# Listing experts in groups of three blocks, halving mask chunks on POOL, and an output tile finished in steps

## The chip, the cores and the metric

The kernel runs on one core of a Trainium2 chip. The metric is the device time of one execution in microseconds (us), as the median of several runs. A profile of one execution, with its trace, tells what each engine did.

## The reference

Two transformer blocks are applied to 256 tokens of width 2048. The change lies in the last part of the second block, a mixture of 16384 single-vector experts with product keys, and in the norm behind it. Each token picks 16 experts for each of 8 heads, so 128 of them:

```
s1, s2 = q[..., :half] @ keys1, q[..., half:] @ keys2
expert, gate = top 16 of all sums of the two top 16 lists, softmax
z = einsum('cd,ced->ce', x, u[expert])
out = einsum('ce,ced->cd', gelu(z) * gate, v[expert])
result = rmsnorm(x + out, norm_final_g)
```

The kernel does not gather `u`: it multiplies all tokens with all 16384 rows of `u`. Of `v` it reads only those rows that some token picked.

## The kernel before

All large products go through one stream of items. An item is a 1 MB weight tile (`raw`, three buffers, loaded on the SP queue) of two halves, and each half is a half-step of the loop in `stream`. In half-step k, ACT cuts the upper part of half k+3 (`whi`, L414), then `step` runs background tasks, then DVE cuts the rest of half k+3 (`wlo`, L421, which also issues the load of a later item), and then PE multiplies half k (L465 and L466: eight products of 512 columns and eight of 256). All engines take their instructions in the order in which they are written, so a background instruction stands at a fixed place between the cuts and products.

`step` deals out background work by a credit: each half-step adds 1.3, a task's `yield c` takes |c| away, a yield of zero or above ends the task's turn in this half-step, and a negative one lets it go on while credit is left. A debt is carried over.

In the part at hand the stream's items are numbered by the 128 tiles of `peer_u` (merged form, L465 and L466), half-step 2i for the first half of tile i, and after them 108 items of `v` (L1645 to L1647). Behind each second tile of `peer_u`, `post_u` closes the pair: ACT copies part of the result (L335), DVE does two operations (L338, L339), ACT a Gelu (L1566) and a store of 256 KB to the table `zg` in memory.

`mask_task(ti)` runs for each 128 tokens; for the second 128 it begins at tile 96, half-step 192. It loads the gates, 128 x 128 cells for 128 tokens, in eight chunks of 1 MB (`vraw<-zg`, L1424, four buffers, on the SP queue between the loads of `raw`), and DVE reduces each with a maximum (L1434). For the second half, `list_task` follows. From the masks it makes three classes of experts (picked by the first tokens only, by both, by the second only), of at most 29, 50 and 29 blocks of 128 list places. A scan on DVE and a small product on PE (L1452) give each picked expert its place. Then pieces of up to five blocks (`PIECE`) are made: POOL (L1489) and DVE (L1490) make a one-hot of the places, PE multiplies it with the counts in groups of at most three blocks (L1504, into one of two PSUM banks `bg`), and the group is evicted. For the first two classes ACT copies a row (L1517) and does one Sign with a sum for each block (L1519); for the third DVE compares and sums (L1510 to L1514). At the end the list positions are ready (L1529), and a flag is set.

`row_source(v)` gathers the rows of `v` by the lists, on POOL's queue (L1603). It is called seven items ahead. If the flag is not set by then, it calls `step` until it is, so that all that is left of the lists is written at one place: ahead of PE's half-step 240. `fetch` gathers rows of `zg` (L1611, six buffers, `ROWS`), and `weigh` multiplies them. PE sums both output tiles in PSUM. The last five items belong to the second tile alone; at the first of them `finish_tile(0)` writes the whole end of the first tile at once: four squares on ACT, the root, four scalings on ACT, four products with the gain on POOL, four stores. `finish_tile(1)` does the same for the second tile after the last item, with DVE for the scaling.

Of the kernel before, what the change touches and what calls it, by code (L numbers as in the profile page):

```python
# [8 lines left out]
F32R = mybir.dt.float32r  # L9
# [5 lines left out]
ALU = mybir.AluOpType  # L15
AX = mybir.AxisListType

P = 128
# [27 lines left out]
    "consts2": [("keep", 384), ("cen", 128)],  # L46
    "consts3": [("tri", 128), ("slots", 640), ("past", 128), ("row", 2), ("starts", 24)],
}
# [3 lines left out]
NLIST = sum(CAPS)  # L52
PIECE = 5
DUMMY = P * P
# [3 lines left out]
EARLY = 3  # L58
ROWS = 6
COEF = 6  # L60
# [15 lines left out]
def constants():  # L76
    c = {}
    r = np.arange(P)
    c["ident"] = np.eye(P)
    half, rot = 8, 16  # L80
    inv = np.power(np.float32(500000.0), -np.arange(half, dtype=np.float32) * np.float32(2.0) / np.float32(rot))
    ang = np.arange(TOK, dtype=np.float32)[None, :] * inv.astype(np.float32)[:, None]
    cos, sin = np.ones((P, TOK)), np.zeros((P, TOK))
    prot = np.zeros((P, P))
    for b in (0, 64):
        for i in range(half):
            cos[b + i] = cos[b + half + i] = np.cos(ang[i])
            sin[b + i] = sin[b + half + i] = np.sin(ang[i])
            prot[b + half + i, b + i] = -1.0
            prot[b + i, b + half + i] = 1.0  # L90
    c["cos"], c["sin"], c["prot"] = cos, sin, prot
    c["blk"] = (r[:, None] // 64 == r[None, :] // 64)
    c["iota"] = np.broadcast_to(r[None, :], (P, P))
    q, k = r[:, None], r[None, :]
    c["keep"] = np.concatenate([k <= q, np.ones((P, P), bool), k <= q], 1)
    c["win"] = np.where(np.concatenate([k <= q, k > q, k <= q], 1), 0.0, NEG)
    cen = np.zeros((P, P))
    for m in range(P):
        cen[:64, m] = -1.0 / 64
        cen[m % 64, m] += 1.0  # L100
    c["cen"] = cen
    c["tri"] = r[:, None] < r[None, :]
    c["slots"] = np.broadcast_to(np.arange(640)[None, :], (P, 640))
    c["past"] = np.zeros((P, P))
    for at, n in zip(CLASS_AT, CAPS):
        c["past"][:, at:at + n] = P * np.arange(n)[None, :] + r[:, None] + 0.5 - P * n / 2
    c["past"][:, :CLASS_AT[2]] *= -1.0
    starts = [P * b for n in CAPS for b in range(0, n, PIECE)]
    c["starts"] = np.broadcast_to(np.array(starts + [0] * (24 - len(starts)))[None, :], (P, 24))
    c["row"] = np.stack([(r - 128.0) * 128.0, 0.0 * r], 1)  # L110
    return {g: np.ascontiguousarray(np.concatenate([c[n].astype(np.float32) for n, _ in items], 1))
            for g, items in _CONSTS.items()}
# [133 lines left out]
class Build:  # L246
# [988 lines left out]
    def peer(self):  # L1235
# [144 lines left out]
        def begin_lists():  # L1380
# [17 lines left out]
            for name, (o, w) in offsets.items():  # L1398
                self.cons[name] = c3[:, o:o + w]
            st["abs"], st["gt"] = cut(2, 640), cut(2, 3, P)  # L1400
            st["hot"], st["prer"] = self.t([2, 640], "hot", dt=F32R), self.t([3, 132], "pre", dt=F32R)
            st["scratch"] = t[:, 0:at[0]]
            st["m"], st["cls"], st["pre"] = cut(2, P), cut(3, P), cut(3, 132)
            st["n"], st["mid"], st["half"], st["end"] = (cut(3) for _ in range(4))
            st["bias"], st["high"] = cut(24), cut(24)
            st["sum"], st["row"], st["rho"] = cut(NLIST), cut(NLIST), cut(NLIST)
# [8 lines left out]
        def mask_task(ti):  # L1415
# [13 lines left out]
            for g in range(3):  # L1429
                load(g)  # L1430
                yield 0.0
            for g in range(8):
                load(g + 3)
                V.tensor_reduce(st["m"][:, ti, 16 * g:16 * g + 16], chunks[g], axis=AX.X, op=ALU.max)  # L1434
                yield 2.3
            V.tensor_scalar(st["m"][:, ti], st["m"][:, ti], 0.0, None, op0=ALU.is_gt)
# [4 lines left out]
        def list_task():  # L1441
# [7 lines left out]
            V.tensor_copy(st["n"], pre[:, :, P - 1])  # L1449
            yield 2.2  # L1450
            ps = self.bg1()
# [5 lines left out]
            for c in range(3):  # L1457
                V.tensor_scalar(pre[:, c, 0:P], pre[:, c, 0:P], ps[:, c:c + 1], -64.0 * CAPS[c], op0=ALU.add, op1=ALU.add)
            V.tensor_scalar(st["prer"][:, :, 0:P], pre[:, :, 0:P], 4096.0, None, op0=ALU.min)
            V.tensor_copy(st["prer"][:, :, P:P + 2], self.con("row")[:, None, :].to_broadcast([P, 3, 2]))  # L1460
            over = st["bias"][:, 0:3]
# [3 lines left out]
            V.tensor_copy(st["over"][:, 0:1], over[:, 0:1])  # L1465
            yield 2.6
            pieces = [(c, b, min(PIECE, CAPS[c] - b)) for c in range(3) for b in range(0, CAPS[c], PIECE)]
            signs, counts = [p for p in pieces if p[0] < 2], [p for p in pieces if p[0] == 2]
            pieces = []
            while signs or counts:  # L1470
                pieces += signs[:3] + counts[:1]
                del signs[:3], counts[:1]
            lo, hi = st["bias"], st["high"]
# [19 lines left out]
            hot(0)  # L1493
            yield -1.0
            for i, (c, b, n) in enumerate(pieces):
                if i + 1 < len(pieces):
                    hot(i + 1)
                    yield -0.6
                for j0 in range(0, n, 3):
                    ps = self.bg1()  # L1500
                    m = min(3, n - j0)
                    for j in range(m):
                        o = (j0 + j) * P
                        T.matmul(ps[:, 132 * j:132 * j + 130], st["hot"][:, i % 2, o:o + P], st["prer"][:, c, 0:130],  # L1504
                                 start=True, stop=True)
                    yield 0.0
                    col = CLASS_AT[c] + b + j0
                    pv = ps[:, 0:396].rearrange("p (b k) -> p b k", k=132)
                    if c == 2:
                        V.tensor_copy(st["row"][:, col:col + m], pv[:, 0:m, P])  # L1510
                        gt = st["gt"][:, j0 // 3 % 2, 0:m]
                        V.tensor_tensor(gt, pv[:, 0:m, 0:P], self.con("past", col, col + m)[:, :, None].to_broadcast([P, m, P]),
                                        op=ALU.is_gt)
                        V.tensor_reduce(st["sum"][:, col:col + m], gt, axis=AX.X, op=ALU.add)  # L1514
                        yield -1.2
                        continue
                    S.activation(st["row"][:, col:col + m], pv[:, 0:m, P], AF.Copy)  # L1517
                    for j in range(m):
                        S.activation(pv[:, j, 0:P], pv[:, j, 0:P], AF.Sign, bias=self.con("past", col + j, col + j + 1),  # L1519
                                     accum_out=st["sum"][:, col + j:col + j + 1])  # L1520
                    yield -0.5
            rho = st["rho"]
            n = CLASS_AT[2]
            V.tensor_scalar(rho[:, :n], st["sum"][:, :n], -0.5, P / 2 + float(DUMMY), op0=ALU.mult, op1=ALU.add)
            V.tensor_scalar(rho[:, n:], st["sum"][:, n:], -1.0, P + float(DUMMY), op0=ALU.mult, op1=ALU.add)
            V.tensor_tensor(rho, rho, st["row"], op=ALU.add)
# [160 lines left out]
        def finish_tile(ti):  # L1687
# [3 lines left out]
            for fb in range(4):  # L1691
                S.activation(junk, acc[fb], AF.Square, accum_out=sq[:, fb:fb + 1])
            V.tensor_reduce(sq[:, 4:5], sq[:, 0:4], axis=AX.X, op=ALU.add)
            r = self.rstd(sq[:, 4:5], 1.0 / D, 1)
            for fb in range(4):
                cs = slice(512 * fb, 512 * (fb + 1))
                if ti:
                    V.scalar_tensor_tensor(st["out"][:, cs], acc[fb], r, st["gain"][:, cs], op0=ALU.mult, op1=ALU.mult)
                else:
                    S.activation(st["out"][:, cs], acc[fb], AF.Copy, scale=r)  # L1700
                    G.tensor_tensor(st["out"][:, cs], st["out"][:, cs], st["gain"][:, cs], op=ALU.mult)
                self.nc.sync.dma_start(A["out"][ti * P:(ti + 1) * P, cs], st["out"][:, cs])

        def v_emit(v):
            def emit(half, hi, lo):
                if half == 0:
# [4 lines left out]
                    if v == NLIST - 12:  # L1711
                        st["gain"], st["out"] = (self.x[:, a:a + 8].rearrange("p c t -> p (c t)") for a in (0, 8))
                        self.nc.sync.dma_start(st["gain"], A["gain"])
                    if v == final[0] + 1:
                        finish_tile(0)
                else:
# [9 lines left out]
        for v in range(NLIST):  # L1726
            items.append((row_source(v), v_emit(v), (lambda: finish_tile(1)) if v == NLIST - 1 else None))
        return items
# [18 lines left out]
```

## Time and profile before

| | us |
|---|---|
| median of 3 runs | 2531.33 |
| lowest and highest | 2530.48, 2532.58 |
| the profiled execution | 2532.76 |
| its span, first to last instruction | 2531.0 |
| PE busy in the span | 2460.1 (97%) |
| DVE busy | 1787.4 (71%) |
| ACT busy | 1364.6 (54%) |
| POOL busy | 792.9 (31%) |

PE is busy nearly all the time, so the time is PE's work, plus the stretches in which PE waits, plus what a lower clock behind such a wait costs. The mean granted clock of the span is 0.986 of full. In the views, an idle time in front of an instruction stands in brackets with what ended it.

### The profile page before, as it was taken

The page shows a single profiled execution, that of the slowest core. Times are in us where ns is not written, and L with a number is a line of the kernel's source. Part 1 is how long each engine was busy: PE and PEld are TensorE (multiplying, and loading weights), DVE is VectorE, ACT ScalarE, POOL GpSimd, SP SyncE. Part 2 cuts the span into 40 slices and gives each one's busy share as a digit, 9 for nine tenths or more (in the row PEclk, how much of TensorE's full clock was granted, in tenths as well). Part 3 has the DMA queues.
Part 4 walks back from the last instruction along what each step waited for, and adds up shares of the span by engine and source line. Part 5 has one row for each costly group of instructions (what it writes and reads, how often), then busy time and mean ns, then how long its engine had stood idle before and what let it go on. Part 6 is the DMA issues. An engine that isn't in the chain of part 4 may idle for free.

```text
span 2531.0 us, 37147 instructions
## 1 busy us (share of the span) xinstructions
PE 2460.1 (97%) x14276; PEld 2157.5 (85%) x14276; DVE 1787.4 (71%) x2818; ACT 1364.6 (54%) x2000; POOL 792.9 (31%) x503
## 2 busy tenths in 40 slices
PE   9999999999999999999999999999989789999997
PEld 8888888899888888889999888878877678778885
DVE  7677777776766787767989655665676557777776
ACT  6566555564556667745354544444435545555554
POOL 0000000000000000000888877777312325556553
PEclk9999999999999999999999999999999799999998
DMA  6545565565543665554677777997874458888884
GB/s 249 183 158 176 187 216 196 197 217 187 190 166 138 227 208 197 173 207 169 171 199 196 233 202 219 245 285 206 257 250 168 157 211 317 317 317 317 317 318 161
DMA packets 180294, 550.88 MB, mean 218 GB/s; under 512 B 47633, under 2 KB 113553, under 8 KB 124050
## 3 DMA queue, kind: packets, MB, share of 16 engines
q1 hardware_dynamic: 101650, 389.99, 45.0%
q0 software_dynamic: 61056, 141.72, 19.1%
q10 hardware_dynamic: 17408, 16.78, 1.9%
q8 instruction: 112, 1.84, 0.3%
q14 instruction: 68, 0.56, 0.1%
HBM read 512.65 MB, written 35.78 MB: 217 GB/s over the span
## 4 chain that ended last, share of the span: by engine, by line
PE 69%; issue 12%; POOL 7%; DMA 4%; DVE 4%; ACT 3%; SPq 0%; POOLq 0%; ACTq 0%; DVEq 0%
PE mm L465 35%; PE mm L466 18%; POOL lists L1611 4%; PE mm L457 3%; PE mm L459 3%; PE mm L458 3%; DMA raw<-peer_u 2%; DVE wlo L421 2%; POOL vraw L1603 2%; POOL raw L1603 1%; ACT whi L414 1%; DMA vraw<-zg 1%; ACT bg L1519 1%; PE bg L1163 1%; DMA raw<-w_in 0%
## 5 line engine op out<-in xcount | busy, mean ns | idle before, releaser
L465 PE MATMUL mm<-act,whi 128*128 128x512 f32 x4368 | 1226.5, 398 | 9.8 <-ACT whi L414 7.4
L421 DVE TENSOR_TENSOR wlo<-raw,whi 128x1024 fp32r<-128x1024 f32 x752 | 901.7, 1223 | 233.1 <-ACT whi L414 162.3
L465 PEld LDWEIGHTS mm<-act,whi 128*128 128x128 f32 x4368 | 792.5, 190 | 135.3 <-ACT whi L414 10.0
L1357 POOL DMA_INDIRECT zg<-sel,at x256 | 477.6, 1866 | 1320.0 <-DMA raw<-w_pq 1204.6
L414 ACT ACTIVATE whi<-raw 128x1024 fp32r<-128x1024 f32 x752 | 759.8, 1049 | 161.5 <-PE mm L465 42.8
L466 PEld LDWEIGHTS mm<-act,wlo 128*128 128x128 f32 x4368 | 674.1, 190 | 69.1 <-DVE wlo L421 2.8
L466 PE MATMUL mm<-act,wlo 128*128 128x256 f32 x4368 | 700.1, 283 | 0.5 <-DVE wlo L421 0.2
L457 PE MATMUL mm<-act,whi 128*128 128x256 f32 x768 | 218.1, 284 | 0.0
L459 PE MATMUL mm<-act,wlo 128*128 128x256 f32 x768 | 217.5, 283 | 0.2 <-DVE wlo L421 0.2
L458 PE MATMUL mm<-act,whi 128*128 128x256 f32 x768 | 217.3, 283 | 0.0
L335 ACT ACTIVATE z<-mm 128x512 f32<-128x512 f32 x107 | 63.7, 596 | 266.8 <-PE mm L465 266.7
L338 DVE TENSOR_TENSOR z<-z,mm 128x512 f32<-128x512 f32 x107 | 73.3, 685 | 156.6 <-ACT z L335 153.7
L421 DVE TENSOR_TENSOR wlo<-vraw,whi 128x1024 fp32r<-128x1024 f32 x126 | 151.0, 1229 | 39.3 <-ACT whi L414 36.1
L1621 ACT ACTIVATE parts<-lists 128x256 fp32r<-128x256 f32 x108 | 45.1, 418 | 204.4 <-DVE lists L1619 204.4
L459 PEld LDWEIGHTS mm<-act,wlo 128*128 128x128 f32 x768 | 146.9, 191 | 0.5 <-DVE wlo L421 0.4
L458 PEld LDWEIGHTS mm<-act,whi 128*128 128x128 f32 x768 | 147.0, 191 | 0.2
L457 PEld LDWEIGHTS mm<-act,whi 128*128 128x128 f32 x768 | 147.0, 191 | 0.0
L1645 PE MATMUL mm<-whi,parts 128*128 128x512 f32 x316 | 125.0, 396 | 13.6 <-ACT parts L1621 8.5
L1646 PE MATMUL bg<-wlo,parts 128*128 128x512 f32 x316 | 126.8, 401 | 1.7 <-DVE wlo L421 1.7
L1611 POOL DMA_INDIRECT lists<-zg,lists x108 | 117.3, 1086 | 34.2 <-issue 32.6
L1646 PE MATMUL mm<-wlo,parts 128*128 128x512 f32 x316 | 124.6, 394 | 2.9 <-DVE wlo L421 2.9
L414 ACT ACTIVATE whi<-vraw 128x1024 fp32r<-128x1024 f32 x126 | 126.9, 1044 | 0.9 <-ACT z L1566 0.5
(330 smaller groups left out, 2627.5 us busy)
## 6 DMA issues: line engine op xcount, KB each, us to landing
raw<-peer_u SPq DMA_DIRECT2D x128, 1024.0 KB
raw<-w_in SPq DMA_DIRECT2D x50, 1024.0 KB
raw<-w_rnn SPq DMA_DIRECT2D x48, 1024.0 KB
zg<-zero SPq DMA_DIRECT2D x16, 1024.0 KB
raw<-w_out SPq DMA_DIRECT2D x16, 1024.0 KB
raw<-w_ple_gate SPq DMA_DIRECT2D x16, 1024.0 KB
raw<-w_q SPq DMA_DIRECT2D x16, 1024.0 KB
raw<-w_o SPq DMA_DIRECT2D x16, 1024.0 KB
```

Of the source, the lines that this page charges most:

```text
L414: self.S.activation(hi, raw[i][:, half * HALF:(half + 1) * HALF], AF.Copy)
L421: self.V.tensor_tensor(lo, raw[i][:, half * HALF:(half + 1) * HALF], cut[k][0].bitcast(F32), op=ALU.subtract)
L457: self.T.matmul(ps, wh, ah, start=first, stop=False)
L458: self.T.matmul(ps, wh, al, start=False, stop=False)
L459: self.T.matmul(ps, wl, ah, start=False, stop=last)
L465: high = lambda i: self.T.matmul(ps, hi[:, ws[i]], both[i], start=(first and i == 0), stop=(last and i == n - 1))
L466: low = lambda i: self.T.matmul(ps[:, 0], lo[:, ws[i]], both[i][:, 0], start=False, stop=False)
L1357: d = G.indirect_dma_start(cells, bass.IndirectOffsetOnAxis(st["at"][:, ti, k:k + 1], 0), st["sel"][:, 2, ti, k:k + 1], None, bounds_check ...
L1603: G.indirect_dma_start(raw, None, A["peer_v"], bass.IndirectOffsetOnAxis(st["vat"][:, b:b + 1], 0), bounds_check=DUMMY - 1, oob_is_err=True)
L1611: d = G.indirect_dma_start(st["zg"][:, v % ROWS].rearrange("p n t -> p (n t)"), None, rows, bass.IndirectOffsetOnAxis(st["zat"][:, b:b + 1 ...
L1645: T.matmul(ps, ch[:, ts], hi, start=False, stop=False)
L1646: T.matmul(ps, ch[:, ts], lo, start=False, stop=False)
```

## The change

The pieces become groups of three blocks in the order of the classes (37 instead of 22). Each piece is one round: one-hot of the next piece, three products, and, in the next round, one row copy and one Sign of 384 columns on ACT into `gt`, and one sum on DVE. To allow one bias for the whole group, five (now three) copies of the counts are kept that are shifted by 128 each. In the second mask, POOL adds the two halves of each chunk's tokens before DVE reduces, which then has 1024 columns instead of 2048. The yields are set anew: 1.25 instead of 2.3 for a chunk, -1.2 instead of 2.2 after the scan, 1.2 instead of 2.6 after the counts, 0.9 a piece. `finish_tile` becomes a task with five stops, the second tile's output has its own place, its last quarter goes by ACT and POOL, and `ROWS` is 7.

```diff
-PIECE = 5
+PIECE = 3
-ROWS = 6
+ROWS = 7
...
+            def half(g):
+                if ti and g < 8:
+                    chunk, chunks[g] = chunks[g], chunks[g][:, :, 0:P // 2]
+                    G.tensor_tensor(chunks[g], chunks[g], chunk[:, :, P // 2:P], op=ALU.add)
+
+            half(0)
+            yield 0.0
             for g in range(8):
                 load(g + 3)
+                half(g + 1)
                 V.tensor_reduce(st["m"][:, ti, 16 * g:16 * g + 16], chunks[g], axis=AX.X, op=ALU.max)
-                yield 2.3
+                yield 1.25 if ti else 2.3
...
             V.tensor_copy(st["n"], pre[:, :, P - 1])
-            yield 2.2
+            yield -1.2
...
-            V.tensor_scalar(st["prer"][:, :, 0:P], pre[:, :, 0:P], 4096.0, None, op0=ALU.min)
-            V.tensor_copy(st["prer"][:, :, P:P + 2], self.con("row")[:, None, :].to_broadcast([P, 3, 2]))
+            for j in range(PIECE):
+                V.tensor_scalar(st["prer"][:, j, :, 0:P], pre[:, :, 0:P], 4096.0, -128.0 * j, op0=ALU.min, op1=ALU.add)
+                V.tensor_copy(st["prer"][:, j, :, P:P + 2], self.con("row")[:, None, :].to_broadcast([P, 3, 2]))
...
-            yield 2.6
+            yield 1.2
...
             for i, (c, b, n) in enumerate(pieces):
                 if i + 1 < len(pieces):
                     hot(i + 1)
-                    yield -0.6
...
+                ps = self.bg1()
+                for j in range(n):
+                    T.matmul(ps[:, 130 * j:130 * j + 130], st["hot"][:, i % 2, j * P:(j + 1) * P], st["prer"][:, j, c],
+                             start=True, stop=True)
+                yield 0.9
+                col = CLASS_AT[c] + b
+                pv = ps[:, 0:390].rearrange("p (b k) -> p b k", k=130)
+                gt = st["gt"][:, i % 2, 0:n]
+                S.activation(st["row"][:, col:col + n], pv[:, 0:n, P], AF.Copy)
+                S.activation(gt, pv[:, 0:n, 0:P], AF.Sign, bias=self.con("past", col, col + 1))
+                V.tensor_reduce(st["sum"][:, col:col + n], gt, axis=AX.X, op=ALU.add)
...
                 S.activation(junk, acc[fb], AF.Square, accum_out=sq[:, fb:fb + 1])
+                if fb % 2:
+                    yield 0.0
             V.tensor_reduce(sq[:, 4:5], sq[:, 0:4], axis=AX.X, op=ALU.add)
             r = self.rstd(sq[:, 4:5], 1.0 / D, 1)
+            yield 0.0
+            out = st["second"] if ti else st["out"]
...
-                        finish_tile(0)
+                        self.spawn(finish_tile(0))
```

## Rows read from the trace of the kernel before

**Rows 1.** The page, costliest groups: DVE's cut (busy us, mean ns | idle before):

```profile
L421 DVE TENSOR_TENSOR wlo<-raw,whi 128x1024 fp32r<-128x1024 f32 x752 | 901.7, 1223 | 233.1 <-ACT whi L414 162.3
```

**Rows 2.** Busy us by stretch: PE, PEld, DVE, ACT, POOL, clock, DMA share, GB/s:

```profile
1840.00:1860.00 20.00, 17.77 (x99) 14.59 (x98) 14.26 (x11) 7.25 (x8) 0.00 (x0) 1.00 1.09 355
...
1900.00:1920.00 20.00, 17.79 (x92) 15.27 (x91) 10.46 (x13) 11.69 (x35) 4.86 (x3) 0.86 0.47 163
```

**Rows 3.** Timeline of PE, second mask and lists: start, us, instruction [idle before]:

```profile
1825.64 0.88 PE L466 MATMUL mm<-act,wlo 128*128 128x256 f32 x6
...
1828.44 0.88 PE L466 MATMUL mm<-act,wlo 128*128 128x256 f32 x6
...
1871.91 0.59 PE L1452 MATMUL bg<-lists 128*128 128x3 f32 x2 [5.10 <-DVE lists L1449]
...
1898.78 0.90 PE L1504 MATMUL bg<-pre,hot 128*128 128x130 f32 x3 [3.15 <-ACT bg L1519]
...
1912.03 0.54 PE L1504 MATMUL bg<-pre,hot 128*128 128x130 f32 x2 [2.21 <-ACT bg L1519]
...
1941.00 0.55 PE L1504 MATMUL bg<-pre,hot 128*128 128x130 f32 x3 [2.82 <-ACT bg L1519]
...
1967.82 0.44 PE L1504 MATMUL bg<-pre,hot 128*128 128x130 f32 x2 [2.20 <-ACT bg L1519]
...
1970.95 0.45 PE L1504 MATMUL bg<-pre,hot 128*128 128x130 f32 x3
...
1974.11 0.33 PE L1504 MATMUL bg<-pre,hot 128*128 128x130 f32 x2
...
1982.63 0.69 PE L1504 MATMUL bg<-pre,hot 128*128 128x130 f32 x2 [5.06 <-ACT bg L1519]
...
2006.60 2.87 PE L465 MATMUL mm<-act,whi 128*128 128x512 f32 x6
```

**Rows 4.** Timeline of the SP queue, second mask:

```profile
1843.07 5.68 SPq L406 DMA_DIRECT2D raw<-peer_u  x1
1848.84 0.39 SPq L1424 DMA_DIRECT2D vraw<-zg  x1
```

**Rows 5.** Timeline of ACT, second mask and one pair's end:

```profile
1861.61 1.06 ACT L414 ACTIVATE whi<-raw 128x1024 fp32r<-128x1024 f32 x1 [4.38 <-DMA raw<-peer_u]
...
1962.50 0.60 ACT L335 ACTIVATE z<-mm 128x512 f32<-128x512 f32 x1 [3.39 <-PE mm L465]
1964.58 0.63 ACT L1566 ACTIVATE z<-z 128x512 f32<-128x512 f32 x1 [1.48 <-DVE z L339]
...
1965.67 1.06 ACT L414 ACTIVATE whi<-raw 128x1024 fp32r<-128x1024 f32 x1 [0.46 <-ACT z L1566]
...
1966.82 0.34 ACT L1519 ACTIVATE bg<-bg,lists 128x128 f32<-128x128 f32 x1
```

**Rows 6.** Groups by line and shape (busy us, mean ns | idle before):

```profile
L1489 POOL TENSOR_SCALAR lists<-lists 128x640 f32<-128x640 f32 x20 | 42.0, 2107 | 153.5 <-ACT whi L414 86.7 <-DVE hot L1490 66.8
L1434 DVE TENSOR_REDUCE lists<-vraw 128x16 f32<-128x2048 f32 x16 | 36.5, 2280 | 4.1 <-DMA vraw<-zg 4.1
...
L1490 DVE SCALAR_TENSOR_TENSOR hot<-lists 128x640 fp32r<-128x640 f32 x20 | 19.0, 958 | 7.3 <-POOL lists L1489 5.3 <-PE bg L1504 2.0
...
L1701 POOL TENSOR_TENSOR xres<-xres 128x512 f32<-128x512 f32 x4 | 5.9, 1512 | 12.7 <-ACT xres L1700 12.7
...
L1514 DVE TENSOR_REDUCE lists<-lists 128x3 f32<-128x384 f32 x6 | 3.3, 553 | 0.2
```

**Rows 7.** Timelines of PE and of ACT, last items:

```profile
2506.40 0.79 PE L1645 MATMUL mm<-whi,parts 128*128 128x512 f32 x1 [4.82 <-ACT whi L414]
...
2498.73 0.58 ACT L1692 ACTIVATE nacc<-mm 128x512 f32<-128x512 f32 x1
...
2514.43 2.94 ACT L414 ACTIVATE whi<-vraw 128x1024 fp32r<-128x1024 f32 x3
```

**Rows 8.** Timeline of DVE, a cut while POOL works (POOL's L1489 began at 1899.53):

```profile
1899.70 1.70 DVE L421 TENSOR_TENSOR wlo<-raw,whi 128x1024 fp32r<-128x1024 f32 x1 [0.27 <-ACT whi L414]
```

More of the change, by code (lines that the diff above doesn't have):

```diff
@@ L46 @@
     "consts2": [("keep", 384), ("cen", 128)],
-    "consts3": [("tri", 128), ("slots", 640), ("past", 128), ("row", 2), ("starts", 24)],
+    "consts3": [("tri", 128), ("slots", 384), ("past", 128), ("row", 2), ("starts", 40)],
 }
@@ L102, in constants @@
     c["tri"] = r[:, None] < r[None, :]
-    c["slots"] = np.broadcast_to(np.arange(640)[None, :], (P, 640))
+    c["slots"] = np.broadcast_to(np.arange(384)[None, :], (P, 384))
     c["past"] = np.zeros((P, P))
@@ L106, in constants @@
         c["past"][:, at:at + n] = P * np.arange(n)[None, :] + r[:, None] + 0.5 - P * n / 2
-    c["past"][:, :CLASS_AT[2]] *= -1.0
+    c["past"] *= -1.0
     starts = [P * b for n in CAPS for b in range(0, n, PIECE)]
-    c["starts"] = np.broadcast_to(np.array(starts + [0] * (24 - len(starts)))[None, :], (P, 24))
+    c["starts"] = np.broadcast_to(np.array(starts + [0] * (40 - len(starts)))[None, :], (P, 40))
     c["row"] = np.stack([(r - 128.0) * 128.0, 0.0 * r], 1)
@@ L1399, in begin_lists @@
                 self.cons[name] = c3[:, o:o + w]
-            st["abs"], st["gt"] = cut(2, 640), cut(2, 3, P)
-            st["hot"], st["prer"] = self.t([2, 640], "hot", dt=F32R), self.t([3, 132], "pre", dt=F32R)
+            st["abs"], st["gt"] = cut(2, PIECE * P), cut(2, PIECE, P)
+            st["hot"], st["prer"] = self.t([2, PIECE * P], "hot", dt=F32R), self.t([PIECE, 3, 130], "pre", dt=F32R)
             st["scratch"] = t[:, 0:at[0]]
@@ L1404, in begin_lists @@
             st["n"], st["mid"], st["half"], st["end"] = (cut(3) for _ in range(4))
-            st["bias"], st["high"] = cut(24), cut(24)
+            st["bias"], st["high"] = cut(40), cut(40)
             st["sum"], st["row"], st["rho"] = cut(NLIST), cut(NLIST), cut(NLIST)
@@ L1465, in list_task @@
             V.tensor_copy(st["over"][:, 0:1], over[:, 0:1])
-            yield 2.6
+            yield 1.2
             pieces = [(c, b, min(PIECE, CAPS[c] - b)) for c in range(3) for b in range(0, CAPS[c], PIECE)]
[L1468 to L1472, printed above, removed]
             lo, hi = st["bias"], st["high"]
@@ L1493, in list_task @@
             hot(0)
-            yield -1.0
+            yield -0.4
             for i, (c, b, n) in enumerate(pieces):
@@ L1497, in list_task @@
                     hot(i + 1)
-                    yield -0.6
[L1499 to L1521, printed above, removed]
@@ L1522, in list_task @@
+                S.activation(gt, pv[:, 0:n, 0:P], AF.Sign, bias=self.con("past", col, col + 1))
+                V.tensor_reduce(st["sum"][:, col:col + n], gt, axis=AX.X, op=ALU.add)
             rho = st["rho"]
-            n = CLASS_AT[2]
-            V.tensor_scalar(rho[:, :n], st["sum"][:, :n], -0.5, P / 2 + float(DUMMY), op0=ALU.mult, op1=ALU.add)
-            V.tensor_scalar(rho[:, n:], st["sum"][:, n:], -1.0, P + float(DUMMY), op0=ALU.mult, op1=ALU.add)
+            V.tensor_scalar(rho, st["sum"], -0.5, P / 2 + float(DUMMY), op0=ALU.mult, op1=ALU.add)
@@ L1692, in finish_tile @@
                 S.activation(junk, acc[fb], AF.Square, accum_out=sq[:, fb:fb + 1])
+                if fb % 2:
+                    yield 0.0
             V.tensor_reduce(sq[:, 4:5], sq[:, 0:4], axis=AX.X, op=ALU.add)
             r = self.rstd(sq[:, 4:5], 1.0 / D, 1)
+            yield 0.0
+            out = st["second"] if ti else st["out"]
             for fb in range(4):
                 cs = slice(512 * fb, 512 * (fb + 1))
-                if ti:
-                    V.scalar_tensor_tensor(st["out"][:, cs], acc[fb], r, st["gain"][:, cs], op0=ALU.mult, op1=ALU.mult)
-                else:
-                    S.activation(st["out"][:, cs], acc[fb], AF.Copy, scale=r)
-                    G.tensor_tensor(st["out"][:, cs], st["out"][:, cs], st["gain"][:, cs], op=ALU.mult)
-                self.nc.sync.dma_start(A["out"][ti * P:(ti + 1) * P, cs], st["out"][:, cs])
+                if ti and fb < 3:
+                    V.scalar_tensor_tensor(out[:, cs], acc[fb], r, st["gain"][:, cs], op0=ALU.mult, op1=ALU.mult)
+                else:
+                    S.activation(out[:, cs], acc[fb], AF.Copy, scale=r)
+                    G.tensor_tensor(out[:, cs], out[:, cs], st["gain"][:, cs], op=ALU.mult)
+                self.nc.sync.dma_start(A["out"][ti * P:(ti + 1) * P, cs], out[:, cs])
+                if fb % 2:
+                    yield 0.0
         def v_emit(v):
@@ L1712, in emit @@
                         st["gain"], st["out"] = (self.x[:, a:a + 8].rearrange("p c t -> p (c t)") for a in (0, 8))
+                        st["second"] = st["zg"].rearrange("p v n t -> p (v n t)")[:, 0:D]
                         self.nc.sync.dma_start(st["gain"], A["gain"])
                     if v == final[0] + 1:
-                        finish_tile(0)
+                        self.spawn(finish_tile(0))
                 else:
@@ L1726, in peer @@
         for v in range(NLIST):
-            items.append((row_source(v), v_emit(v), (lambda: finish_tile(1)) if v == NLIST - 1 else None))
+            items.append((row_source(v), v_emit(v), (lambda: self.spawn(finish_tile(1))) if v == NLIST - 1 else None))
         return items
```

## The prediction

> **What bounds the kernel now.** I read first how much of the span PE is busy, and by stretches of 20 us where it isn't. The span is 2531.0 us in a profiled execution of 2532.76, so 1.8 us lie around it. Before the second mask and in the stream of `v` rows PE has work at full clock, and nothing of the change touches it there. What the change can move is PE's waiting between half-step 192, where the second mask begins, and half-step 240, ahead of which the lists must be written, and the waiting in the last five items. So I read the waits of PE one by one next [rows 3], then for each what ended it: the SP queue [rows 4] and ACT [rows 5, 7].
>
> Three kinds stand there. In the mask the DMA is the limit: its share is 1.09 at 355 GB/s [rows 2], and the load queue takes turns of one weight tile and one chunk, 6.2 us for the 2 MB of such a turn (the last chunk is issued 5.8 us after the tile ahead of it began [rows 4]), while ACT sits 4.38 us for a tile that lands at 1861.6 [rows 5]. The mask ends in a wait of 5.10 us, at the product that needs the scan; it starts at 1871.9, ahead of half-step 211. In the lists four waits of 2.2 to 3.2 us stand behind a closed pair, each for ACT's eviction of a group. And from 1982.6 on, behind a wait of 5.06, the rest of the lists is written in one burst; half-step 240 starts only at 2006.6 [rows 3].
>
> **The rhythm.** A bare half-step lasts 2.80 us (1825.64 to 1828.44). With three list products it lasts 3.16 (1970.95 to 1974.11), so a list product costs 0.12 where PE has other work [rows 3].
>
> **Part 1, the mask.** DVE's reduction of 2048 columns takes 2.28 us [rows 6]; half the columns are half of that, 1.15. POOL's addition has 1024 columns; 512 take 1.27 alone and 1.51 on average [rows 6], so 2.5 to 3.0, and I take 2.5, since POOL is idle there. That saves DVE 8 x 1.13 = 9 us, but DVE isn't what the mask waits for. What counts is the new yield. With 1.3 a half-step, 2.3 a chunk gave eight chunks in 13 half-steps and the scan's product at 211; 1.25 gives one in each half-step, and as scan and product now fall into one turn, the product stands at 205. The loads do not come sooner for that: they are the same bytes in nearly the same order. Before, the tile issued just behind the last chunk lands at 1861.6, so at 3.1 us a MB the chunk landed at about 1858.5; now it stands ahead of one more tile, so 1855.4. Behind it come POOL 2.5, DVE's maximum 1.15, a cut 1.2, the closed pair's two operations on DVE (1.4), Gelu and store on ACT until ACT may cut again (1.1), that cut 1.05, DVE's cut 1.2 [rows 1, 5], and mask, scan and copies 2.0 (an estimate from eight small operations). That is 1867.0, and each of these is queued, so nothing passes it. Each reduction that waits for its chunk now also holds DVE's cuts behind it, for which PE waits. So PE is at its scan product 4.9 us earlier (1871.9 - 1867.0), but six half-steps, 16.8 us of work, are then still to be done: 11.9 us lost. Bounds: if the chunks landed as soon as DVE asked, nothing is lost; with POOL at 3.0 and slower landing 16.
>
> *A page on this.* By the Trainium skill, GPSIMD Engine Reference, 3.1 Elementwise, an addition of 2048 columns takes 4497 ns on GPSIMD, and 2293 on VectorE; half of it is an estimate of 2.25 us for the chunk, which would move the sum by 0.25. The trace's L1701 [rows 6] speaks for a little more.
>
> **Part 2, the pieces.** ACT has less to do: per three blocks a Sign of 384 columns, about 0.51 by the lengths for 128 and 512 columns (0.34 and 0.60 [rows 5]), instead of three at 0.34, each with its sum read out behind it. DVE has more: a sum of 0.55 [rows 6] for 37 pieces, 20 us, and a one-hot of about 0.60 (958 ns for 640 columns [rows 6]). POOL's one-hot part shrinks from 2.1 to about 1.3 [rows 6] and lies beside. Neither engine becomes the bound: PE needs 3.16 a half-step, DVE 1.2 + 0.5 + 0.6 and its share of a pair, 0.35, so 2.65.
>
> The order of the work counts more. Behind a pair's end at time t, ACT holds its copy from t+0.2 (1962.50), Gelu (1964.58) and the next cut (from 1965.67); the eviction's first Sign starts 4.5 us after t (1966.82) [rows 5]. Before, PE waited until the group was evicted, and the one-hot was already made. Now DVE's sum stands behind the Sign, and the one-hot of the piece after next behind the sum: t + 4.5 + 0.5 + 0.55 + 0.6 = t + 6.2. PE, through the products of the next piece and a half-step, is there at t + 3.16. So each closed pair costs 3.04 us, where the four like it cost 2.2 to 3.15 [rows 3], and now it happens at every pair, not at those alone that evict through ACT. One piece a half-step from 208 on meets seven such pairs up to 240: 21.3 us. The first one-hot falls behind a pair's end too, DVE's operations and 0.6, so 3.1 us. Bounds for a pair: 2.2 (eviction alone, as at 1967.82) and 3.6 (the one-hot with POOL in its way).
>
> **Part 3, the burst.** By the new yields 33 pieces are made by half-step 240, and four are left, instead of ten of five blocks. The first of them waits until t + 6.2, the others take about 1.6 each (Sign, sum, one-hot and product one behind the other, two pieces in turn), so half-step 240 starts at t + 10.4, of which 9.0 are idle.
>
> **Part 4, the clock.** In the stretch 1900 to 1920 the granted clock is 0.86 [rows 2]; there lie the consequences of the waits at 1898.78 and 1912.03, three products taking 0.90 where they take 0.55 behind 1941.00 [rows 3]. 20 x 0.14 / 2 = 1.4 us for each fall, and two of four such waits had one. I take four of eight: 5.6 us (0 to 11). Behind the scan's wait it falls as before: 2.0.
>
> *The sum for the lists,* from the scan's product to half-step 240. Before: 1871.9 to 2006.6. After: 1867.0 + 0.9 for the product + 35 x 2.80 = 98.0 + 108 x 0.12 = 13.0 + 2.0 + 3.1 + 21.3 + 9.0 + 5.6 = 2019.9, so 13.3 us later. From there to the last five items I see no change: gathers of `v` follow the flag as before, and a seventh buffer of table rows helps where no wait stands (0 to 1.3 us more for one issue).
>
> **Part 5, the end.** PE waits 4.82 us at 2506.40 for a cut that stands behind the first tile's whole end on ACT [rows 7]. In steps, cuts stand between the squares and scalings. All ACT's work in front of the last cut stays, but it no longer sits idle behind DVE: from 2498.73, where the first square began [rows 7], six cuts of 1.06, four squares and four scalings of 0.6 with their sums and gaps (5.4 in all), two weighings (0.8) and some 2.8 of waits for DVE give a last cut done near 2514.1 instead of 2517.4 (2514.43 + 2.94) [rows 7], and PE, not slowed by the clock, follows 0.9 us closer. With one scaling of the last tile moved from DVE to ACT and POOL, 0.3: a gain of 4.5 us (2 to 7).
>
> So 13.3 - 4.5 = 8.8 us more: 2541.6 for the profiled execution, which is 1.4 above the median; from the median 2531.33 it is 2540.
>
> **Rivals.** *The mask hides its earlier asking* (no change): if chunks land sooner because the loads are asked for sooner, the 11.9 us of part 1 go, and the time is 2528, within 0.2%. For it: DMA was not full at every moment before the mask. Against: the share of 1.09 from one end of the mask to the other. *The pairs don't wait* (faster): if the eviction were done before the pair's copy, so that one-hots are ready, the 24.4 us of part 2 and the 5.6 of the clock go: 2510; if half of the pairs escape, 2525. For it: pairs whose groups DVE evicted show no such wait before. Against: now all groups go through ACT. *DVE becomes the bound by sharing with POOL* (slower still): a cut beside POOL's one-hot took 1.70 us [rows 8] instead of 1.22 [rows 1]. If all of 37 pieces meet one such, 0.5 x 37 = 18 us of DVE; it decides as soon as DVE's half-step passes PE's 3.16, and 2.65 + 0.5 is just there. I price it at half, 9 to 11 us: 2551. The Trainium skill, GPSIMD Engine Reference, 1 Specifications, says that the SBUF interfaces are shared with VectorE, with contention where its instruction has two SBUF inputs; the trace's 1.70 agrees, and by that rule the new addition on POOL would slow cuts too. *The end doesn't come in steps in time* (2545): the task's five stops just fit into five half-steps.
>
> **Chances.** My forecast has 0.48, DVE as bound (and the late end) 0.12, so slower by over 0.2% 0.60; 0.2% is 5 us, about what a measurement of this kernel can tell from no change. The hidden mask with 0.23 is the same, the escaped pairs 0.17 are faster. The range reaches from 2526, half of the pairs escaping or the mask's loss gone, to 2552, DVE in the way or all clocks falling.
>
> **What would show it.** Right: PE's scan product (L1452) near 1867 with a wait of over 10 us in front; waits of about 3 us for DVE's one-hot at each pair in the lists; a burst of four pieces; half-step 240 near 2020; in the end no wait over 2 us. Wrong: a scan product before 1860, list waits of under 1 us, or half-step 240 before 2007.

## The result and the profile after

The changed kernel takes **2548.2 us** (six runs, 2547.12 to 2549.55), the kernel before beside it 2531.95: a ratio of 1.0063 with a 95% interval of 1.0050 to 1.0076. It is slower by 16.2 us; forecast were 2540, within 2526 to 2552. The profiled execution took 2548.56 us, of which 2546.8 are span.

The page of the changed kernel, its first lines:

```profile
span 2546.8 us, 37080 instructions
...
PE 2459.6 (97%) x14276; PEld 2157.4 (85%) x14276; DVE 1790.3 (70%) x2836; ACT 1346.9 (53%) x1885; POOL 828.1 (33%) x527
```

PE has as much work as before (2459.6 us for 2460.1), ACT 18 us less and POOL 35 us more, but neither of these two bounds the kernel: nothing in the totals shows 16 us. The order of the work does. Four places are the same point of the program, or nearly, in both kernels (start of the instruction, us):

| | before | forecast | after |
|---|---|---|---|
| product behind the scan | 1871.91, ahead of half-step 211 | 1867.0, ahead of 205 | 1865.92, ahead of 205 |
| half-step 240 | 2006.60 | 2019.9 | 2026.51 |
| first product of the `v` stream | 2069.32 | | 2088.33 |
| end of the span | 2531.0 | 2539.8 | 2546.8 |

The timeline of PE in the changed kernel, second mask and lists (start, us, instruction, in brackets the idle time before it and what ended it); it answers to [rows 3]:

```profile
1865.92 0.58 PE L1460 MATMUL bg<-lists 128*128 128x3 f32 x2 [15.17 <-DVE lists L1457]
...
1880.54 0.55 PE L1504 MATMUL bg<-pre,hot 128*128 128x130 f32 x3 [2.67 <-DVE hot L1494]
...
1899.46 0.87 PE L1504 MATMUL bg<-pre,hot 128*128 128x130 f32 x3 [2.91 <-DVE hot L1494]
...
1916.60 0.66 PE L1504 MATMUL bg<-pre,hot 128*128 128x130 f32 x2 [2.77 <-DVE hot L1494]
...
1933.73 0.87 PE L1504 MATMUL bg<-pre,hot 128*128 128x130 f32 x3 [2.91 <-DVE hot L1494]
...
2004.04 0.52 PE L1504 MATMUL bg<-pre,hot 128*128 128x130 f32 x3 [2.90 <-DVE hot L1494]
...
2021.25 0.88 PE L1504 MATMUL bg<-pre,hot 128*128 128x130 f32 x3 [5.76 <-DVE hot L1494]
...
2026.51 2.82 PE L465 MATMUL mm<-act,whi 128*128 128x512 f32 x6
```

PE stands 15.17 us for the scan. Then come seven waits of 2.77 to 2.91, one behind each pair (1950.95, 1969.65 and 1986.92 are left out here), and each is ended by DVE's one-hot. At four of the seven the list products themselves already take 0.87 for 0.52 (or 0.66 for two of them): the clock has fallen. At the other three it falls a little later, as PE's rows behind the wait of 2.91 at 1969.65 show:

```profile
1969.65 0.52 PE L1504 MATMUL bg<-pre,hot 128*128 128x130 f32 x3 [2.91 <-DVE hot L1494]
1970.01 1.92 PE L465 MATMUL mm<-act,whi 128*128 128x512 f32 x6
1971.73 1.48 PE L466 MATMUL mm<-act,wlo 128*128 128x256 f32 x6
```

The six products at 1971.73 take 1.48 us, at full clock 0.88 [rows 3].

The chain behind one pair, read from ACT and then DVE of the changed kernel; it answers to [rows 5]:

```profile
1910.71 0.60 ACT L335 ACTIVATE z<-mm 128x512 f32<-128x512 f32 x1 [4.69 <-PE mm L465]
...
1912.80 0.63 ACT L1555 ACTIVATE z<-z 128x512 f32<-128x512 f32 x1 [1.48 <-DVE z L339]
...
1913.88 1.06 ACT L414 ACTIVATE whi<-raw 128x1024 fp32r<-128x1024 f32 x1 [0.46 <-ACT z L1555]
...
1914.90 0.57 ACT L1511 ACTIVATE lists<-bg,lists 128x384 f32<-128x384 f32 x1
```
```profile
1915.51 0.55 DVE L1512 TENSOR_REDUCE lists<-lists 128x3 f32<-128x384 f32 x1 [2.74 <-ACT lists L1511]
1915.98 0.47 DVE L1494 SCALAR_TENSOR_TENSOR hot<-lists 128x256 fp32r<-128x256 f32 x1
```

Copy, Gelu, cut, Sign, sum, one-hot: the one-hot at 1915.98 needs nothing of the sum at 1915.51, it only stands behind it on DVE, and PE's product at 1916.60 follows it.

The stretches of 20 us in the changed kernel (busy us of PE, PEld, DVE, ACT, POOL, then clock, DMA share, GB/s); they answer to [rows 2]:

```profile
1840.00:1860.00 20.00, 6.39 (x32) 4.73 (x32) 10.17 (x10) 4.66 (x6) 11.13 (x4) 0.88 0.93 295
...
1900.00:1920.00 20.00, 17.23 (x85) 14.67 (x85) 13.30 (x20) 8.43 (x17) 9.28 (x6) 0.84 0.43 134
1920.00:1940.00 20.00, 17.09 (x95) 14.86 (x95) 12.39 (x17) 8.73 (x17) 8.80 (x6) 0.91 0.45 156
1940.00:1960.00 20.00, 17.09 (x87) 14.92 (x86) 11.63 (x16) 7.61 (x15) 6.85 (x5) 0.83 0.40 126
```

Of the granted clock there are two levels, 1.2 and 2.4 GHz, so 0.83 means that the lower one held for a third of the stretch. Before, the one at 0.86 [rows 2] was the only such stretch between 1900 and 1980, where the other three stood at 1.00; now each of the five from 1900 to 2000 is at 0.83 to 0.91.

### The profile page after: what moved, and what is told of

It is laid out like the page before. It is cut to its first block, busy times and chain, and to the rows that moved or that the text cites. A ratio compares the mean times of both kernels' runs of the same rounds, so it can differ in the third digit from the quotient of the medians.

```text
span 2546.8 us, 37080 instructions
## 1 busy us (share of the span) xinstructions
PE 2459.6 (97%) x14276; PEld 2157.4 (85%) x14276; DVE 1790.3 (70%) x2836; ACT 1346.9 (53%) x1885; POOL 828.1 (33%) x527
## 4 chain that ended last, share of the span: by engine, by line
PE 74%; issue 9%; POOL 5%; DVE 4%; DMA 4%; ACT 3%; SPq 0%; ACTq 0%; POOLq 0%; DVEq 0%
PE mm L465 35%; PE mm L466 18%; PE mm L457 3%; PE mm L458 3%; PE mm L459 3%; POOL lists L1600 3%; DVE wlo L421 2%; ACT whi L414 1%; DMA vraw<-zg 1%; POOL vraw L1592 1%; DMA raw<-peer_u 1%; POOL raw L1592 1%; PE mm L1635 1%; PE bg L1635 1%; PE mm L1636 1%
## 5 line engine op out<-in xcount | busy, mean ns | idle before, releaser
L1357 POOL DMA_INDIRECT zg<-sel,at x256 | 471.8, 1843 | 1320.4 <-DMA raw<-w_pq 1205.3
```

Of the source, the lines that this page charges most:

```text
L1357: d = G.indirect_dma_start(cells, bass.IndirectOffsetOnAxis(st["at"][:, ti, k:k + 1], 0), st["sel"][:, 2, ti, k:k + 1], None, bounds_check ...
```

## The experiments

Each median stands beside that of the kernel before, taken with it, then the ratio with its 95% interval. Where 2531.27 stands beside, the recorded ratio isn't quite the quotient of the two medians (1.0021 for the filled waits). The kernel before took 2531.27, 2533.53 and 2532.99 in three sets of runs, so times of different sets compare to about 2 us.

**The end alone.** The kernel before, with the stepwise end, the place of the second output and the last quarter on ACT and POOL, and nothing else:

```diff
+                if fb % 2:
+                    yield 0.0
...
-                        finish_tile(0)
+                        self.spawn(finish_tile(0))
```

> The kernel before, with the stepwise end of both output tiles alone. Theory: the end is worth 4.3 us by itself (half-step 240 is 20.1 us later in the changed kernel, the span only 15.8), so 2527.6, with no wait of PE over 2 us in the last five items. Rival: the end gains nothing by itself and the later lists gave the 4.3 us back in the stream of v rows; then 2532 as before.

Measured: 2527.29 beside 2531.27, ratio 0.9976 (0.9964 to 0.9987). The largest wait of PE in the last items, from its timeline in this kernel:

```profile
2505.97 0.50 PE L1646 MATMUL mm<-wlo,parts 128*128 128x512 f32 x1 [1.32 <-DVE wlo L421]
```

It stands where 4.82 us stood [rows 7]. Part 5 is right, with 4.0 us for its 4.5.

**The mask's pace undone.** The changed kernel with the old yields in the mask and behind the scan; POOL still halves the chunks:

```diff
-                yield 1.25 if ti else 2.3
+                yield 2.3
...
-            yield -1.2
+            yield 2.2
```

> The changed kernel with the pace of the kernel before in the second mask: 2.3 a chunk and 2.2 behind the scan, POOL's halving kept. Theory: the 15.17 us wait at the scan's product comes from asking early for chunks that DMA can't deliver sooner. The product then stands at half-step 212 with a wait of about 5 us, pieces begin seven half-steps later, two pair waits fewer (9 us with the clock), a burst of 11 pieces instead of 4 (11 us more): half-step 240 near 2014 instead of 2026.7, total near 2536. Rival: POOL's halving or the scan's own length makes the wait; then it stays over 12 us and the total is 2548 or, with the longer burst, 2555.

Measured: 2534.98 beside 2531.27, ratio 1.0013 (1.0004 to 1.0023). The timeline of PE in this kernel:

```profile
1869.53 0.39 PE L1460 MATMUL bg<-lists 128*128 128x3 f32 x2 [2.61 <-DVE lists L1457]
...
2013.14 2.87 PE L465 MATMUL mm<-act,whi 128*128 128x512 f32 x6
```

The wait for the scan falls from 15.17 to 2.61, with the product ahead of half-step 212 instead of 205, and although the lists start later and eleven pieces instead of four are left for the burst, half-step 240 starts 13.4 us earlier than in the changed kernel. These 13.4 are a net figure. The product comes 3.6 us later, but with seven half-steps more, 19.6 us of work, already done: 16.0 won. After the product 2.6 are lost again, since the longer burst costs more than the one pair wait that falls away (six instead of seven; the expectation had two fewer). So the denser asking costs as part 1 says: it moves PE's wait ahead of work that could have covered it.

**Halving alone.** The kernel before with POOL's halving of the second mask and no other yields:

```diff
+                half(g + 1)
                 V.tensor_reduce(st["m"][:, ti, 16 * g:16 * g + 16], chunks[g], axis=AX.X, op=ALU.max)
```

> The kernel before with POOL's halving of the second mask's chunks alone, paces as before. Theory: DVE's shorter reductions don't bring the chunks sooner, but at the unhurried pace they shorten what stands between the last chunk and the scan's product, so its wait falls from 5.1 to about 2.6 us, and the total by 2 to 3 us, 2529. Rival: POOL's additions slow DVE's cuts by sharing, and the wait stays at 5 or grows; 2531 to 2534.

Measured: 2534.62 beside 2533.53, ratio 1.0004 (0.9994 to 1.0013); the expectation of a gain failed. From the timeline of PE in this kernel:

```profile
1872.97 0.59 PE L1459 MATMUL bg<-lists 128*128 128x3 f32 x2 [6.12 <-DVE lists L1456]
```

The product comes 1.06 us later than before, and the wait grew, as the rival had it. For a chunk that has landed, POOL's 2.42 and DVE's 1.22, one behind the other, are a longer way than DVE's 2.28 alone: the last reduction ends at 1863.30, before at 1862.80. But that is not what the product waits for. The cut behind the reduction stands another 0.46 for ACT's cut, and ACT for its weight tile:

```profile
1862.67 1.06 ACT L414 ACTIVATE whi<-raw 128x1024 fp32r<-128x1024 f32 x1 [5.53 <-DMA raw<-peer_u]
```

Before, this cut starts at 1861.61 [rows 5], the whole 1.06 earlier, and from it to the scan's product it is 10.30 us in both kernels. Why the tile lands later isn't isolated. POOL's additions do hold up DVE's cuts, as the rival says, and loads of later items are issued behind these cuts: two cuts that begin at 1827.98, 0.14 us behind an addition of 2.40, take 4.47 together, where two take 2.35 at 1857.44. The time that DVE saves lies beside this and helps nobody.

**The eviction in the turn of its products.** The changed kernel with one line moved, so that copy, Sign and sum are written in the same half-step as the products, ahead of the next pair's copy and of the next one-hot:

```diff
-                yield 0.9
                 col = CLASS_AT[c] + b
...
                 V.tensor_reduce(st["sum"][:, col:col + n], gt, axis=AX.X, op=ALU.add)
+                yield 0.9
```

> The changed kernel with each piece's eviction written in the turn of its products, ahead of the pair's end, instead of in the next turn. Theory: the 2.9 us at each pair are the chain pair copy, Gelu, cut, Sign, sum, one-hot. With the Sign ahead of the pair's copy, one-hots are ready; the wait falls to about 1.1 (the sum behind the next cut), the clock falls at no pair or few: 8 x (1.8 + 1.5) and about 3 in the burst, so 29 us less: 2519. Rival: DVE or POOL are short of time anyhow (their sharing), and the waits stay near 2.9: 2545 to 2548.

Measured: 2522.02 beside 2531.27, ratio 0.9951 (0.9932 to 0.9971), so 26 us less than the changed kernel. PE's timeline and a stretch of this kernel:

```profile
1929.38 0.52 PE L1504 MATMUL bg<-pre,hot 128*128 128x130 f32 x3 [0.89 <-DVE hot L1494]
...
2000.80 1.59 PE L465 MATMUL mm<-act,whi 128*128 128x512 f32 x3
```
```profile
1920.00:1940.00 20.00, 19.11 (x116) 16.76 (x115) 14.16 (x20) 9.62 (x18) 7.47 (x6) 1.00 0.51 179
```

The pairs' waits are 0.77 to 1.03, the clock is full, and half-step 240 starts 25.7 us earlier. Seven waits shorter by 2 us are 14 of it; the rest is mostly clock, which the next two runs separate from the waits.

**The waits filled.** The changed kernel with twelve products of 512 columns ahead of those list products that wait, into a bank that nobody reads, so PE has work in the waits (an addition to the computation that leaves the output as it is):

```diff
+                if i % 4 == 1 and 4 < i < 33:
+                    extra = self.bg2()
+                    for r in range(FILL):
+                        T.matmul(extra[:, r % 2], st["prer"][:, 0, 0, 0:P],
```

> The changed kernel with twelve more products of 512 columns (about 2.8 us at full clock) written ahead of the seven list products that wait for a one-hot behind a pair, into a bank that nobody reads. They take the place of the idle time, and the one-hots come no sooner. Theory: each of these waits also makes the granted clock fall, worth about 1.5 us each; with the products in the waits the clock stays and the time falls by 7 to 10 us, to 2538 to 2541, though PE has more to do. Rival: the half-steps behind the waits are long for another reason (DVE, DMA); then the time stays at 2548 or rises by what the products exceed the waits.

Measured: 2536.63 beside 2531.27, ratio 1.0011 (1.0002 to 1.0021). PE's timeline and a stretch of this kernel:

```profile
1881.63 0.55 PE L1511 MATMUL bg<-pre,hot 128*128 128x130 f32 x3 [2.66 <-DVE hot L1495]
...
2015.45 2.87 PE L466 MATMUL mm<-act,whi 128*128 128x512 f32 x6
```
```profile
1900.00:1920.00 20.00, 19.89 (x114) 16.87 (x113) 14.35 (x22) 10.09 (x21) 12.33 (x6) 1.00 0.44 144
```

The clock is 1.00 in each of the five stretches from 1900 to 2000. The chains behind the pairs are what they were, PE has more to do, and the kernel is 11.6 us faster than the changed one. From the first piece to half-step 240 (1881.63 to 2015.45) it takes 133.8 us, the changed kernel 146.0 (1880.54 to 2026.51): **12.2 us of the changed kernel's time are the clock behind its seven pair waits**, 1.7 each.

**The one-hot ahead of the eviction.** The changed kernel with the one-hot of piece i+2 written behind the products of piece i and ahead of its eviction, so that it no longer stands behind the sum:

```diff
+            hot(1)
...
-                if i + 1 < len(pieces):
-                    hot(i + 1)
...
+                if i + 2 < len(pieces):
+                    hot(i + 2)
```

> The changed kernel with the one-hot of the piece after next written ahead of the eviction in the same turn, so that it stands behind no sum; the eviction itself stays behind the pair's copy. It tells the two halves of the 2.9 us apart. Theory: the Sign comes too late (its PSUM bank) and the sum and one-hot behind it come on top; then the waits fall to about 2.0, ended by the bank's Sign, as at 2.2 in the kernel before. If the clock still falls at each, 8 x 0.9 less: 2541; if it falls at half of them, 2535. Rival: the one-hot is late for its own reasons (POOL, DVE's cuts); then the waits stay at 2.9 and the total at 2548.

Measured: 2532.33 beside 2533.53, ratio 0.9994 (0.9984 to 1.0003), better than expected. PE's timeline and two stretches of this kernel:

```profile
1929.10 0.55 PE L1503 MATMUL bg<-pre,hot 128*128 128x130 f32 x3 [1.70 <-ACT lists L1512]
```
```profile
1920.00:1940.00 20.00, 18.30 (x103) 15.96 (x102) 13.55 (x18) 7.38 (x14) 6.70 (x6) 0.91 0.51 179
1940.00:1960.00 20.00, 16.60 (x100) 14.24 (x99) 12.63 (x18) 10.53 (x20) 6.21 (x5) 1.00 0.38 132
```

Each wait is now 1.70 and ended by ACT's Sign, which frees the PSUM bank. So of the 2.91 the sum and one-hot on DVE are 1.2, and the late eviction the rest. The clock fell behind only about half of these waits (0.91 in three of the five stretches, 1.00 in two); that is why 1.2 us less in each of seven waits gave 15.9 us.

**Both mended.** The old pace of the mask, the eviction in its turn, and -0.85 a piece, so that more pieces are done before half-step 240:

```diff
-                yield 0.9
...
+                yield -0.85
```

> The changed kernel with both causes taken away: the pace of the kernel before in the second mask, evictions in the turn of their products, and -0.85 a piece, so that one and a half pieces go into each half-step and the lists still end by half-step 240. Theory: scan product near 1870 ahead of half-step 212 with 2.6 us, 28 half-steps of 2.80, 13 for products, pair waits of 1 to 1.6 without a fall of the clock, a short burst: half-step 240 near 1985 instead of 2006.6 before, total near 2506. Rival: with 1.5 pieces a half-step DVE (1.2 + 0.35 + 1.5 x 1.15 = 3.3 us) or ACT is the bound and PE waits in each half-step; then 28 x 0.5 to 1.0 more, 2520 to 2535.

Measured: 2521.89 beside 2533.53, ratio 0.9957 (0.9941 to 0.9974): no better than the moved eviction alone, 16 us above the expectation. DVE, PE and a stretch of this kernel:

```profile
1928.09 0.55 DVE L1511 TENSOR_REDUCE lists<-lists 128x3 f32<-128x384 f32 x1 [2.21 <-ACT lists L1510]
1928.56 1.22 DVE L421 TENSOR_TENSOR wlo<-raw,whi 128x1024 fp32r<-128x1024 f32 x1
1929.69 0.61 DVE L1494 SCALAR_TENSOR_TENSOR hot<-lists 128x384 fp32r<-128x384 f32 x1
```
```profile
1930.45 0.88 PE L1504 MATMUL bg<-pre,hot 128*128 128x130 f32 x3 [3.76 <-DVE hot L1494]
```
```profile
1920.00:1940.00 20.00, 16.24 (x83) 14.27 (x84) 12.46 (x18) 8.67 (x19) 7.44 (x7) 0.83 0.33 119
```

Where a half-step takes two pieces, the sum of the first waits for its Sign, and the one-hot at 1929.69 stands behind it again. Four pair waits are 3.64 to 3.85 and the clock falls at each, which eats what the mask's pace gave. The expectation had priced the pieces' number, not the order within a turn. The rival's time, 2520 to 2535, fits, but not its mechanism: PE waits at the pairs and not in each half-step.

**A third one-hot buffer.** The kernel of the last experiment, with the one-hot two pieces ahead; that takes three buffers:

```diff
-            st["hot"], ... = self.t([2, PIECE * P], "hot", dt=F32R), ...
+            st["hot"], ... = self.t([3, PIECE * P], "hot", dt=F32R), ...
...
+            hot(1)
...
-                if i + 1 < len(pieces):
-                    hot(i + 1)
+                if i + 2 < len(pieces):
+                    hot(i + 2)
```

> The kernel with both mended, with a third one-hot buffer, so that each one-hot is written two pieces ahead and in front of the eviction. In e6_both_mended six waits of 2.5 to 3.9 us are left, most for a one-hot that stands behind the sum of the piece ahead. Theory: with one-hots ready, what is left behind a pair is the bank's Sign, 1.7 us, and the clock falls at half of them or none: 5 x (2.0 + 0.8) = 14 us less, 2508. Rival: with one and a half pieces a half-step ACT or DVE is short of time, and the waits stay at 3 or more, ended by another instruction: 2518 to 2522.

Measured: **2501.69** beside 2532.99, ratio 0.9877 (0.9860 to 0.9893), 6 us better than expected. PE and a stretch of this kernel:

```profile
1925.76 0.55 PE L1505 MATMUL bg<-pre,hot 128*128 128x130 f32 x3 [1.58 <-ACT lists L1511]
...
1975.20 0.67 PE L1505 MATMUL bg<-pre,hot 128*128 128x130 f32 x5
```
```profile
1920.00:1940.00 20.00, 17.65 (x109) 15.50 (x107) 16.29 (x23) 10.64 (x21) 9.94 (x9) 1.00 0.48 172
```

The waits in the rhythm are 1.36 to 1.58, again for the bank, and all pieces are done by 1975.9, so there is no burst at half-step 240. The first product of `v` starts at 2042.03. It differs from the experiment before by the buffer and the one-hot's place alone, and these are worth 20.2 us. This version beats both kernels, the one before by 31.3 us. That isn't the group of three with one Sign alone: the stepwise end is worth 4.0 of it, and no run puts the pieces of five into the same order, so what the groups give by themselves stays open.

## Why the prediction was right, and where it was short

**The sign and the mechanism** were right: a moved wait in the mask, a wait at each pair, a short burst, a small gain in the end. Half-step 240 came 19.9 us later than before instead of 13.3; the span is 15.8 longer, so 4.1 were given back behind it, of 4.5 forecast.

**Part 1.** 1865.92 for 1867.0, ahead of the half-step that was named. Against the kernel before this is 6.0 us earlier with six half-steps, 16.8, still to be done: 10.8 us lost for the 11.9, and the pace as the cause is shown by its undoing. That the place fits so well is in part luck, as two terms erred against each other. POOL took the last chunk at 1853.45 where 1855.4 was worked out, and its addition took 3.38 there instead of 2.5, a cut having begun 0.04 us ahead of it. From POOL and DVE of the changed kernel:

```profile
1849.89 2.35 POOL L1435 TENSOR_TENSOR vraw<-vraw 128x1024 f32<-128x1024 f32 x1 [3.27 <-DMA vraw<-zg]
1853.45 3.38 POOL L1435 TENSOR_TENSOR vraw<-vraw 128x1024 f32<-128x1024 f32 x1 [1.21 <-DMA vraw<-zg]
```
```profile
1852.28 1.22 DVE L1442 TENSOR_REDUCE lists<-vraw 128x16 f32<-128x1024 f32 x1 [3.27 <-POOL vraw L1435]
1853.41 1.22 DVE L421 TENSOR_TENSOR wlo<-raw,whi 128x1024 fp32r<-128x1024 f32 x1
```

The rival that hides the earlier asking falls here too: POOL itself waits for chunks in the DMA, 3.27 and 1.21 us, although they were asked for sooner.

**Part 2.** The pair wait was forecast at 3.04 and is 2.77 to 2.91, seven times (20.2 us for 21.3); the first one-hot at 3.1 and is 2.67. The operations, by the groups of the changed kernel (busy us, mean ns, idle before):

```profile
L1511 ACT ACTIVATE lists<-bg,lists 128x384 f32<-128x384 f32 x34 | 19.8, 585 | 0.0
L1512 DVE TENSOR_REDUCE lists<-lists 128x3 f32<-128x384 f32 x34 | 18.7, 549 | 27.4 <-ACT lists L1511 27.4
L1494 DVE SCALAR_TENSOR_TENSOR hot<-lists 128x384 fp32r<-128x384 f32 x34 | 20.6, 609 | 0.0
L1493 POOL TENSOR_SCALAR lists<-lists 128x384 f32<-128x384 f32 x34 | 58.5, 1731 | 103.9 <-DVE hot L1494 86.8 <-DVE lists L1485 17.1
```

Forecast were 0.51, 0.55, 0.60 and 1.3. Only POOL's mean was far off (one that stands alone, as at 1907.23, takes 1.24), and it lies beside. The rival of pairs that don't wait falls with the seven rows. That of DVE as the bound names something real, for nine of the 33 cuts between 1880 and 2027 take 1.36 to 1.59 us instead of 1.22; but DVE still has 27.4 us of idle time ahead of its sums, and its mean cut over the whole kernel is 1.231, 1.223 before [rows 1].

**Part 3.** The burst has four pieces. With t at 2015.04, where the products behind the pair's end begin, the first of the four starts at t + 6.2, as forecast, and half-step 240 at t + 11.5 instead of t + 10.4: the pieces behind the first were sized too short, 5.3 us for 4.2. (The sum of the prediction has 0.3 more for this burst than its t + 10.4.)

**Part 4 is the step that failed: the clock.** It took a fall behind four of eight waits, 1.4 us each, because before two of four waits had one. In the changed kernel the waits come every 17.4 us on average (1899.46 to 2004.04, six periods), where four half-steps with pieces, 12.64, and the forecast wait make 15.7 at full clock; so each period lost 1.7 us. The filled waits show the cause: 12.2 us went with the idle time, where 5.6 stood in the sum. The difference, 6.6, is as much as half-step 240 came later than forecast; that it is the same figure is chance, as the other terms cancel. The scan is 1.1, the seven pairs 1.1 and the first one-hot 0.4 early. Late are the stretch behind the scan, 0.7 (1865.92 to 1877.87, for three half-steps, 0.9 and 2.0), and the burst, also 0.7 (11.0 from 2015.49, for 9.0 and eleven products), and the clock is low in both; the other 1.3 lie in the rhythm, and no row names their cause. So the count was wrong (all seven, not about half), the size of one fall (1.7 for 1.4) less so. The bound of 11 that the prediction gave for this term was nearer than its middle. With 12.2 in place of 5.6 the forecast would have been 2546.6.

**Part 5.** The largest wait in the last items of the changed kernel:

```profile
2527.00 0.50 PE L1635 MATMUL mm<-wlo,parts 128*128 128x512 f32 x1 [1.34 <-DVE wlo L421]
```

From the first product of `v` to the end it takes 458.5 us, before 461.7: 3.2 of the 4.1 that were given back lie there. Which of the small differences in front of it holds the other 0.9 stays open. The rival of an end that doesn't come in steps falls with the 1.34. A seventh buffer of table rows did nothing to be seen: the wait at the start of `v` is 8.43, 8.46 before.

## What to carry to other kernels

On engines that take their instructions in order, ask of each new operation not only what it costs but what it will stand behind: a one-hot that was ready ahead of time became late because a sum, itself late by a pair's copy, Gelu and cut, was written ahead of it. Asking a saturated queue for data sooner can move the wait to an earlier place in the program and take away the work that could have covered it. A repeated short wait of TensorE can have a price beside its length: where waits of near 3 us come again and again, put a term for the clock behind every one, not behind half of them, and test it by filling the waits with products.

## What the runs showed of the hardware

**The clock.** Waits of 2.77 to 2.91 us, one every 17 us, brought a fall of the granted clock each time; 1.70 about every second time; 1.36 to 1.58, with the third buffer, in one of the four stretches from 1900 to 1980 (0.91 from 1940 to 1960); 0.77 to 1.03, with the eviction moved, in none of these (1.00). A wait of 2.9 us thus cost 4.6. Its length alone doesn't decide, though: in the kernel before, waits of 3.15 and 2.21 brought a fall and 2.82 and 2.20 none [rows 3]; what else counts no run isolates.

**POOL beside DVE.** By the spans of the profile, an addition of 1024 columns on POOL and a cut on DVE held each other up, and the one that began second paid. The addition took 2.35 us while DVE waited for it, and 3.38 where a cut had begun 0.04 us ahead of it; that cut kept its 1.22. In the same kernel it also went the other way:

```profile
1826.56 2.39 POOL L1435 TENSOR_TENSOR vraw<-vraw 128x1024 f32<-128x1024 f32 x1 [1.88 <-DVE wlo L421]
```
```profile
1826.82 3.22 DVE L421 TENSOR_TENSOR wlo<-raw,whi 128x1024 fp32r<-128x1024 f32 x1
```

This cut began 0.26 us behind the addition and ended 1.09 behind its end, so the new addition does slow cuts, as the prediction had it for its rival of sharing. Beside POOL's part of a one-hot the price was smaller: 1.70 instead of 1.22 [rows 8]. The Trainium skill, GPSIMD Engine Reference, 1 Specifications, states the contention for DVE instructions with two SBUF inputs; these rows agree.
